# Down projection of a conv-FFN: separate buffers for the seven-product units, and another order of the units

## The chip, the cores and the metric

The kernel runs on one core of one Trainium2 chip. The metric is the time of one execution on the device in microseconds (us), as the median of several runs. Alongside it stands one profiled execution, whose trace gives every instruction with its start, its duration and what it waited for.

Engines are named as the profile names them: PE (TensorE, matrix products; PEld is its weight load), DVE (VectorE), ACT (ScalarE), POOL (GpSimd) and SP (SyncE, which here only issues DMAs; SPq is its queue).

## The reference

One decoder layer on 256 tokens of width 2048, all in float32: an attention mixer with a residual, then a gated FFN with a causal convolution. Only the second half matters here:

```python
a, b = jnp.split(h @ w_up, 2, axis=-1)          # w_up: 2048 x 11264
c = conv_b + sum(conv_w[j] * ap[:, j:j + S] for j in range(3))
y = (gelu(c) * b) @ w_down                      # w_down: 5632 x 2048
out = x + rms_norm(y, norm_ffn_post)
```

In what follows G stands for `gelu(c) * b`, 256 tokens by 5632 columns, and "down" for the product of G with `w_down`.

## The kernel before

**Numbers.** Each float32 operand is split in two parts, a high part `hi` (float32r, written by ACT with a cast) and a low part `lo` (the difference, written by DVE). A product of two operands is three matmuls (lines 175 to 177): high by high, high by low, low by high. One of them covers 128 rows by 128 columns against 512 columns.

**Weights.** A weight chunk of 128 partitions by 1024 floats (512 KB) goes through four hands. SP issues its load into a tile `raw`, of which there are three (`RAW = 3`, tag "raw"). ACT casts it to `whi` (L143), DVE subtracts to get `wlo` (L144), and PE reads both. Once both L143 and L144 have read a raw tile, it is free for the next load. Of converted pairs (`whi`, `wlo`) five can be outstanding in this stage (four, and one in two flexible tiles). `wchunk` loads and converts in one step. In the down stage the loads are issued by `raw_row` (L151), and `convert` does the other two steps.

**Stages around the change.** `ffn_up(c, ...)` makes 512 columns of G at a time. Columns 1 to 5 are made first, as k-tiles 4 to 23, after column 0 in `ffn_up0`. Then `down_pair(0)` and `down_pair(1)` multiply k-tiles 0 to 23 with `w_down`, each for one half (1024) of its columns, and add the result into `dsum` (tiles `ds`). Then `ffn_up` makes columns 6 to 10 in the same G tiles, and `down` finishes k-tiles 24 to 43, followed by the post-FFN norm with its scale `gpost2` (`z_block`, L1174) and the residual.

**Inside `down_pair`.** Twenty-four k-tiles are twelve units of two k-tiles each. Eight are plain: for each k-tile a row of weights is loaded and converted, and multiplied for two token halves and two column halves, so that a k-tile takes 4 products and a plain unit 24 matmuls. Four units (u = 0 to 3) use a scheme of seven products instead of eight (a Strassen-like one), 21 matmuls. Such a unit loads both its rows (`even`, `odd`), forms four differences of 128x512 on DVE (L1124 to L1127) in two further tiles `ta` and `tb`, and converts `odd`, half of `even`, `ta` and `tb`. Both raw rows are held until the last difference (L1127) and their conversions are done. `PAIR_ORDER` gives the order: `p` a plain unit, `s` a unit of seven. The products go to eight PSUM banks: four are called `c` and collect all units, and four are called `q` and collect products of the seven-units alone. At the last seven-unit of a pair (`if last`) one ACT copy and four DVE adds (L1141 to L1145) move `q` into `dsum`. After the whole pair, four adds (L1155) take in `c`. Pair 1 uses the banks of pair 0 the other way around, and the next `ffn_up` writes first (tile `ua`, L1041) into the banks that were `q` in pair 1.

**What sets the order.** The program is written as steps in the order of PE's work. The framework then gives each engine a fixed order by priority and by its own estimate of when inputs are ready; an instruction can be taken ahead of others where the estimate has its engine idle. On the chip each engine, and SP's queue among them, works through its list in order and stands at a semaphore until the inputs are there. Tiles of one tag follow one another in program order: the next one may be written when all readers of the one before are done.

**The tag "gp".** One tile of 128x2048 floats (1 MB in all). First it holds `gpost`, the scale after the mixer, whose last reader is L858. Then it holds `gpost2`, loaded by one broadcast DMA from POOL (L1077), and first read by L1174.

**x2b.** The residual is parked in DRAM and loaded back by eight DMAs on SP (`unpark`, L1013), each 256 KB. Its tiles are held until then by the token sums `s` of the seven-units, the first for units 0 and 1, the second for units 2 and 3.

Of the kernel before, what the change touches and what calls it, by code (L numbers as in the profile page):

```python
# [19 lines left out]
P = 128  # L20
D = 2048
# [20 lines left out]
def trunk_layer(ctx, tc, x, x_cols_in, conv_cols_in, g_mix_post, g_ffn_post, w_in, w_q, w_kv,  # L42
                sinks, rel, wo_a, wo_b, w_out, w_up, w_down, rope_tab, strip_sel, out):
    nc = tc.nc
    vec, act, pe, pool = nc.vector, nc.scalar, nc.tensor, nc.gpsimd

    def open_pool(name, bufs=1, **kw):
        es = ExitStack()
        return es, es.enter_context(tc.tile_pool(name=name, bufs=bufs, **kw))
# [9 lines left out]
    def sb(pl, shape, name, dt=F32, tag=None, bufs=None):  # L59
        return pl.tile(shape, dt, name=name, tag=tag or name, **({"bufs": bufs} if bufs else {}))  # L60
# [46 lines left out]
    def ring_tile(kind, name, dt, extra):  # L107
        pl_tag = dict(name=name, tag="flex", bufs=2) if extra else dict(name=name, tag=kind, bufs=RAW if kind == "raw" else RING)
        return ring.tile([P, 1024], dt, **pl_tag)

    def in_turn(kind):

        turn[kind] += 1
        return flex[0] == kind and turn[kind] % (RAW + 2 if kind == "raw" else RING + 1) >= (RAW if kind == "raw" else RING)
# [32 lines left out]
    def raw_row(src):  # L147
        i = cnt[0]
        cnt[0] += 1
        raw = ring_tile("raw", f"raw{i}", F32, in_turn("raw"))  # L150
        nc.sync.dma_start(raw, src)  # L151
        return raw
# [4 lines left out]
    def at(t, *fs):  # L157
        steps[max(t, now[0])].extend(fs)
# [20 lines left out]
    def gemm(xh, xl, w, k0, nk, c0, n, split=None, extra=None, ps=None):  # L179

        kc = 1024 // n if n in (256, 512) else 2
        acc = new_acc("g", ps)
        todo = []
        cuts = list(range(0, nk, kc)) + [nk]
        for ci, (k, ke) in enumerate(zip(cuts[:-1], cuts[1:])):
            kk = ke - k
            src = w[(k0 + k) * P:(k0 + k + kk) * P, c0:c0 + n].rearrange("(a p) n -> p a n", p=P)
            hi, lo = wchunk(src, [kk, n], *(extra or {}).get(ci, ()))
            for j in range(kk):
                kt = k + j  # L190
                wh, wl = hi[:, j * n:(j + 1) * n], lo[:, j * n:(j + 1) * n]
                for t in range(NT):
                    x_ = [x(k0 + kt)[:, t * P:(t + 1) * P] for x in (xh, xl)]
                    if split is None or t == 0 or ci < split:
                        mm3(acc[t][:, :n], *x_, wh, wl, kt == 0, kt == (split * kc if split and t else nk) - 1)
                    else:
                        todo.append((kt, x_, wh, wl))
            tick()
        return acc, todo
# [377 lines left out]
    acc, _ = gemm(XH, XL, w_in, 0, KT, 0, 512)  # L577
# [4 lines left out]
    acc, _ = gemm(XH, XL, w_in, 0, KT, C_KV, KVR + ROPE)  # L582
# [201 lines left out]
    for j in range(4):  # L784
        acc, _ = gemm(XH, XL, w_in, 0, KT, C_GA + 512 * j, 512)
# [15 lines left out]
    es6, p6 = open_pool("p6")  # L801
# [33 lines left out]
    for j in range(4):  # L835
        ld = merge_loads(j)
        acc, _ = gemm(AH, AL, wo_a, 0, KT, 512 * j, 512)
# [124 lines left out]
    def ffn_up0():  # L962

        sa = [[None, None], [None, None]]

        def evac(acc, q):
            f = sb(p6, [P, 1024], f"f{q}_0", tag="f" + "ab"[q], bufs=2)
            for t in range(NT):
                a = f[:, t * 512:(t + 1) * 512]
                act.activation(a, acc[t], AF.Copy, scale=rf[t][q][:, 0:1])  # L970
                sa[t][q] = a

        def cols(i):
            pt = pst.tile([P, 512], F32, name=f"fT{i}", tag="t")
            for q in range(2):
                for t in range(NT):
                    pe.transpose(pt[:, q * 256 + t * P:q * 256 + (t + 1) * P], sa[t][q][:, i * P:(i + 1) * P], ident)
            conv_cols(i, pt[:, 0:256], pt[:, 256:512], i)

        acc, todo = gemm(HH, HL, w_up, 0, KT, 0, 512, split=0, extra=first_extra)  # L980
        finish_tile(acc[1], todo)
        x2_norm(0)
        x2_norm(1)
        evac(acc, 0)
        drain()
        es8.close()
        esx.close()
        es7, p7 = open_pool("p7")
        g = [slot("b", i) if i < 8 else sb(p7, [P, 1024], f"ghl{i}", F32R) for i in range(12)]
        gT[0][:], gT[1][:] = highs(g), lows(g)  # L990
        dsum_all[:] = [sb(p7, [P, D], f"ds{t}") for t in range(NT)]
        dsum[:] = [[d[:, j * 512:(j + 1) * 512] for j in range(4)] for d in dsum_all]
        norm_row()
        for p in range(8):
            at(now[0] + 1 + (3 * p) // 2, lambda p=p: normed(p, p7))
        acc, _ = gemm(HH, HL, w_up, 0, KT, DFF, 512, ps=(pss, "s"))
        evac(acc, 1)
        for i, w in enumerate((1, 2, 4, 6)):
            at(now[0] + w, lambda i=i: cols(i))
        gtiles[:] = g  # L1000
        s_pool.append(p7)
        return es7
# [70 lines left out]
            at(now[0] + 1 + 2 * i, lambda i=i: conv_cols(4 * c + i, sa[0][i], sa[1][i], slot0 + i))  # L1073

    es7 = ffn_up0()
    gpost2 = sb(p6, [P, D], "gpost2", tag="gp")
    pool.dma_start(gpost2, g_ffn_post.partition_broadcast(P))  # L1077
    for c in range(1, 6):
        if c == 2:
            for i in range(8):  # L1080
# [15 lines left out]
    def down_pair(p):  # L1096

        c11, c12, c21, c22 = c = banks(p, f"c{p}_")
        q1, q5, q7, q6 = q = banks(1 - p, f"q{p}_")
        j0, used = 2 * p, set()  # L1100
        d = [dsum[t][j0 + j] for t in range(NT) for j in range(2)]
        act_of = lambda k, t: (GH(k)[:, t * P:(t + 1) * P], GL(k)[:, t * P:(t + 1) * P])
        row = lambda k: w_down[k * P:(k + 1) * P, j0 * 512:(j0 + 2) * 512]
        half = lambda w, i: tuple(x[:, i * 512:(i + 1) * 512] for x in w)

        def mul(o, x, w, last=False):
            mm3(o, *x, *w, id(o) not in used, last)
            used.add(id(o))

        def plain(u, last):  # L1110
            for k in (2 * u, 2 * u + 1):
                w = convert(raw_row(row(k)), 1024)
                for t in range(NT):
                    for j in range(2):
                        mul(c[2 * t + j], act_of(k, t), half(w, j), last and k % 2 == 1)
                tick()

        def seven(u, last):
            s1, s2, s3, s4 = s_of[u]
            even, odd = raw_row(row(2 * u)), raw_row(row(2 * u + 1))  # L1120
            ta, tb = (sb(p6, [P, 1024], f"t{n}{p}_{u}", tag="f" + n, bufs=2) for n in "ab")
            lo_, hi_ = slice(0, 512), slice(512, 1024)
            w = convert(odd, 1024)
            vec.tensor_tensor(ta[:, lo_], even[:, hi_], even[:, lo_], op=ALU.subtract)  # L1124
            vec.tensor_tensor(ta[:, hi_], odd[:, hi_], even[:, hi_], op=ALU.subtract)
            vec.tensor_tensor(tb[:, lo_], odd[:, hi_], ta[:, lo_], op=ALU.subtract)
            vec.tensor_tensor(tb[:, hi_], odd[:, lo_], tb[:, lo_], op=ALU.subtract)  # L1127
            mul(c11, act_of(2 * u + 1, 0), half(w, 0))
            mul(c12, s4, half(w, 1))
            w = convert(even, 512)  # L1130
            mul(q1, act_of(2 * u, 0), half(w, 0), last)
            w = convert(ta, 1024)
            mul(q5, s1, half(w, 0), last)
            mul(q7, s3, half(w, 1), last)
            tick()
            w = convert(tb, 1024)
            mul(q6, s2, half(w, 0), last)
            mul(c21, act_of(2 * u + 1, 1), half(w, 1))
            tick()
            if last:  # L1140
                act.copy(d[0], q1)  # L1141
                vec.tensor_tensor(d[1], d[0], q6, op=ALU.add)
                vec.tensor_tensor(d[2], d[1], q7, op=ALU.add)
                vec.tensor_tensor(d[3], d[2], q5, op=ALU.add)
                vec.tensor_tensor(d[1], d[1], q5, op=ALU.add)  # L1145

        plain_of, seven_of = iter(range(4, 12)), iter(range(4))
        for i, kind in enumerate(PAIR_ORDER):
            if kind == "s":
                u = next(seven_of)  # L1150
                seven(u, u == 3)
            else:
                plain(next(plain_of), i == len(PAIR_ORDER) - 1)
        for o, x in zip(d, c):
            vec.tensor_tensor(o, o, x, op=ALU.add)  # L1155

    for p in range(2):
        down_pair(p)
    for i in range(8):
        at(now[0] + 40 + 2 * i, lambda i=i: unpark(i // 4, i % 4))  # L1160
    for c in range(6, 11):
# [65 lines left out]


RING = 4
PAIR_ORDER = "psppsppsppsp"  # L1230
XCUT = [0, 1, 2, 3, 4, 6, 8, 10, 12, 14, 16]
X_LOAD = [0, 1, 2, 3, 4, 6, 7, 8, 10]
X_SQ = [4, 4, 5, 5, 6, 7, 8, 9, 10, 11]
# [71 lines left out]
```

## Time and profile before

| what | value |
|---|---|
| median of 3 runs | 1475.25 us (1474.59 to 1475.66) |
| time of the profiled execution | 1475.35 us |
| span of the profiled execution | 1473.5 us |
| granted TensorE clock | 0.998 |
| down stage, pair 0 (first matmul to first matmul of pair 1) | 1003.91 to 1066.47 us |
| down stage, pair 1 (to the first matmul of the next `ffn_up`) | 1066.47 to 1132.44 us |

All times of the trace count from the start of the span, which lies within the profiled execution's 1475.35 us with 1.85 us around it. In a row of groups the columns are: line, engine, operation, what is written and read, shape and count, then busy time and mean duration of one in ns, then idle time of the engine just before them and what ended it. In a timeline row they are start, duration, engine, line, operation, and in brackets idle time ahead and what released it. Waits give the total in us, how many times, and the longest. Chain rows give the start and the length of each step of the sequence that ended last. Window rows give for each stretch the busy time of PE, PEld, DVE, ACT and POOL with counts, then the granted clock, the DMA engines' busy share and GB/s.

The duration of a matmul in the trace is modelled: one of 512 columns is listed with 0.39 us, though one starts every 0.23 us. PE's busy time therefore hides a part of every short stop; the starts show it.

### The profile page before, as it was taken

Reading aid. Unit: us, or ns where it says so; the run is one execution under the profiler, and the core shown is the slowest. Engines: PE = TensorE matmul, PEld = TensorE weight load, DVE = VectorE, ACT = ScalarE, POOL = GpSimd, SP = SyncE. Lnnn points to the kernel's source line nnn. Section 1 sums busy time; section 2 is a strip of 40 time slices with the busy share of each in tenths; the row PEclk is TensorE's granted clock in tenths of the full one; section 3 lists DMA queues with packets and bytes.
Section 4 is the critical chain, followed back from the end, with each engine's and each line's share of the span. In section 5 each row is a group of like instructions: output and inputs, shape, how many; then the busy total and the mean of one; then the engine's idle time right before and its main releaser. Section 6 shows DMA issues by size and latency. Waiting matters only on the chain.

```text
span 1473.5 us, 20861 instructions
## 1 busy us (share of the span) xinstructions
PE 1460.6 (99%) x7591; PEld 1246.1 (85%) x7591; DVE 1026.6 (70%) x1799; ACT 818.3 (56%) x1354; POOL 51.1 (3%) x87
## 2 busy tenths in 40 slices
PE   9999999999999999999999999999999999999997
PEld 7888888888888888888888888888877888888886
DVE  7788874445667665555799877677777676677556
ACT  7588864444565554444666565555444565565443
POOL 0021100000000010000000000000000000000000
PEclk9999999999999999999999999999999999999999
DMA  8755376666655559755766666665667666666653
GB/s 291 223 171 165 94 219 195 206 209 200 186 160 156 171 163 339 224 197 195 224 202 184 192 193 185 188 196 162 209 199 226 210 200 190 194 186 187 198 189 126
DMA packets 154513, 287.58 MB, mean 195 GB/s; under 512 B 18427, under 2 KB 29596, under 8 KB 154284
## 3 DMA queue, kind: packets, MB, share of 16 engines
q1 hardware_dynamic: 149664, 270.43, 59.4%
q0 software_dynamic: 4656, 15.78, 3.4%
q8 instruction: 59, 0.97, 0.3%
q14 instruction: 42, 0.34, 0.1%
q10 hardware_dynamic: 92, 0.05, 0.0%
HBM read 277.79 MB, written 8.44 MB: 194 GB/s over the span
## 4 chain that ended last, share of the span: by engine, by line
PE 92%; DVE 3%; DMA 3%; ACT 1%; issue 0%; DVEq 0%; ACTq 0%; SPq 0%
PE accg L175 15%; PE accg L177 15%; PE accg L176 15%; PE ub L1041 10%; PE ua L1041 10%; PE ua L1045 5%; PE ub L1045 5%; DMA raw<-in_ffn_w_down_dram 2%; PE c L175 1%; PE c L176 1%; PE c L177 1%; DVE wlo L144 1%; PE mpo L760 1%; PE ms L726 1%; PE pt L442 1%; PE qn L691 1%
## 5 line engine op out<-in xcount | busy, mean ns | idle before, releaser
L144 DVE TENSOR_TENSOR wlo<-raw,whi 128x1024 fp32r<-128x1024 f32 (+2 forms) x502 | 604.7, 1207 | 345.4 <-ACT whi L143 340.6
L143 ACT CAST whi<-raw 128x1024 fp32r<-128x1024 f32 (+2 forms) x502 | 518.6, 1036 | 495.7 <-PE accg L177 239.2
L175 PE MATMUL accg<-whi,ahl 128*128 128x512 f32 (+1 forms) x544 | 212.9, 391 | 0.0
L177 PE MATMUL accg<-whi,ahl 128*128 128x512 f32 (+1 forms) x544 | 210.5, 387 | 0.0
L176 PE MATMUL accg<-wlo,ahl 128*128 128x512 f32 (+1 forms) x544 | 209.7, 385 | 0.0
L175 PE MATMUL accg<-whi,bhl 128*128 128x512 f32 x442 | 173.0, 391 | 0.0
L177 PE MATMUL accg<-whi,bhl 128*128 128x512 f32 x442 | 172.3, 390 | 0.0
L176 PE MATMUL accg<-wlo,bhl 128*128 128x512 f32 x442 | 172.2, 390 | 0.0
L1041 PE MATMUL ua<-ahl,whi 128*128 128x512 f32 x640 | 154.8, 391 | 0.9 <-DVE ds L1145 0.9
L1041 PE MATMUL ub<-ahl,whi 128*128 128x512 f32 x640 | 154.6, 391 | 0.0
L1041 PEld LDWEIGHTS ua<-ahl,whi 128*128 128x128 f32 x640 | 117.4, 188 | 24.0 <-DVE ds L1145 1.3
L1041 PEld LDWEIGHTS ub<-ahl,whi 128*128 128x128 f32 x640 | 117.5, 188 | 22.9 <-ACT cc L930 0.3
L177 PEld LDWEIGHTS accg<-whi,ahl 128*128 128x128 f32 x544 | 102.1, 188 | 20.6
L176 PEld LDWEIGHTS accg<-wlo,ahl 128*128 128x128 f32 x544 | 102.3, 188 | 18.1
L175 PEld LDWEIGHTS accg<-whi,ahl 128*128 128x128 f32 x544 | 102.3, 188 | 17.9
L177 PEld LDWEIGHTS accg<-whi,bhl 128*128 128x128 f32 x442 | 83.0, 188 | 17.4
L175 PEld LDWEIGHTS accg<-whi,bhl 128*128 128x128 f32 x442 | 83.0, 188 | 16.9
L176 PEld LDWEIGHTS accg<-wlo,bhl 128*128 128x128 f32 x442 | 83.0, 188 | 16.8
L1045 PEld LDWEIGHTS ub<-ahl,wlo 128*128 128x128 f32 x640 | 82.2, 191 | 3.2
L1045 PEld LDWEIGHTS ua<-ahl,wlo 128*128 128x128 f32 x640 | 82.2, 191 | 3.1
L1045 PE MATMUL ua<-ahl,wlo 128*128 128x256 f32 x640 | 83.7, 283 | 0.0
L1045 PE MATMUL ub<-ahl,wlo 128*128 128x256 f32 x640 | 83.2, 283 | 0.0
(409 smaller groups left out, 1876.1 us busy)
## 6 DMA issues: line engine op xcount, KB each, us to landing
raw<-in_ffn_w_up_dram SPq DMA_DIRECT2D x176, 512.0 KB, 4.5
raw<-in_w_in_dram SPq DMA_DIRECT2D x111, 512.0 KB, 4.4
raw<-in_ffn_w_down_dram SPq DMA_DIRECT2D x88, 512.0 KB, 4.3
raw<-in_w_o_swa_dram SPq DMA_DIRECT2D x32, 512.0 KB, 4.3
raw<-in_w_o_mla_dram SPq DMA_DIRECT2D x32, 512.0 KB, 4.8
raw<-in_w_out_dram SPq DMA_DIRECT2D x32, 512.0 KB, 4.2
bias<-strip POOLq DMA_DIRECT2D x16, 256.0 KB, 4.3
raw<-in_mla_w_q_up_dram SPq DMA_DIRECT2D x32, 128.0 KB, 2.6
```

Of the source, the lines that this page charges most:

```text
L143: act.copy(hi[:, a:b], raw[:, a:b])
L144: vec.tensor_tensor(lo[:, a:b], raw[:, a:b], hi[:, a:b].bitcast(F32), op=ALU.subtract)
L175: pe.matmul(o, ah, bh, start=start, stop=False)
L176: pe.matmul(o, ah, bl, start=False, stop=False)
L177: pe.matmul(o, al, bh, start=False, stop=stop)
L442: pe.transpose(pt[:, j * P:(j + 1) * P], p[:, c * P:(c + 1) * P], ident)
L691: pe.matmul(o, wl, ch(k), start=False, stop=k == nk - 1)
L726: pe.matmul(o, w, v_, start=n == 0, stop=False)
L760: pe.matmul(o, w(t), p_[:, c], start=n == 0, stop=n == 5)
L1041: pe.matmul(acc[i], hi[:, c], hn[p][:, j * 512:(j + 1) * 512], start=p + j == 0, stop=stop)
L1045: pe.matmul(acc[i][:, 0:256], lo[:, c], hn[p][:, j * 512:j * 512 + 256], start=False, stop=False)
```

## The change

Three edits. First, a unit of seven no longer takes its two rows from the three `raw` tiles. It allocates one tile of 128x2048 with the tag "gp" and loads its two rows into the halves. Second, `gpost2` is allocated and loaded after both pairs, since the same tile serves the eight seven-units in between. Third, `PAIR_ORDER` becomes a pair of orders, one for each column pair. Both end in two plain units; before, both ended in one.

```diff
     es7 = ffn_up0()
-    gpost2 = sb(p6, [P, D], "gpost2", tag="gp")
-    pool.dma_start(gpost2, g_ffn_post.partition_broadcast(P))
     for c in range(1, 6):
...
         def seven(u, last):
             s1, s2, s3, s4 = s_of[u]
-            even, odd = raw_row(row(2 * u)), raw_row(row(2 * u + 1))
+            both = sb(p6, [P, D], f"rr{p}_{u}", tag="gp")
+            even, odd = both[:, 0:1024], both[:, 1024:2048]
+            nc.sync.dma_start(even, row(2 * u))
+            nc.sync.dma_start(odd, row(2 * u + 1))
...
-        for i, kind in enumerate(PAIR_ORDER):
+        for i, kind in enumerate(PAIR_ORDER[p]):
             if kind == "s":
                 u = next(seven_of)
                 seven(u, u == 3)
             else:
-                plain(next(plain_of), i == len(PAIR_ORDER) - 1)
+                plain(next(plain_of), i == len(PAIR_ORDER[p]) - 1)
...
     for p in range(2):
         down_pair(p)
+    gpost2 = sb(p6, [P, D], "gpost2", tag="gp")
+    pool.dma_start(gpost2, g_ffn_post.partition_broadcast(P))
...
-PAIR_ORDER = "psppsppsppsp"
+PAIR_ORDER = ("ppsppspspspp", "psppsppspspp")
```

## Prediction

> **What bounds the kernel now.** I read the page first, then PE in the two column pairs by windows and by its starts, then the waits, then the chain that ended last. The page:
>
> ```profile
> span 1473.5 us, 20861 instructions
> PE 1460.6 (99%) x7591; PEld 1246.1 (85%) x7591; DVE 1026.6 (70%) x1799; ACT 818.3 (56%) x1354; POOL 51.1 (3%) x87
> ```
>
> PE is the bound nearly everywhere, so the change can only win what PE loses in the down stage. Windows of the two pairs, and PE's starts in them:
>
> ```profile
> 1003.91:1066.47 62.56, 62.56 (x278) 51.80 (x276) 50.04 (x63) 32.43 (x40) 0.00 (x0) 1.00 0.60 190
> 1066.47:1134.20 67.73, 65.01 (x281) 51.87 (x279) 49.91 (x57) 31.18 (x33) 0.00 (x0) 1.00 0.65 201
> ```
>
> ```profile
> 1003.91 0.39 PE L175 MATMUL c<-whi,bhl 128*128 128x512 f32 x1
> ...
> 1066.47 0.39 PE L175 MATMUL c<-whi,bhl 128*128 128x512 f32 x1
> ...
> 1076.08 0.50 PE L176 MATMUL q<-wlo,s 128*128 128x512 f32 x1 [0.16 <-DVE wlo L144]
> ...
> 1089.52 0.50 PE L176 MATMUL c<-wlo,bhl 128*128 128x512 f32 x1 [0.82 <-DVE wlo L144]
> ...
> 1122.02 0.50 PE L176 MATMUL c<-wlo,bhl 128*128 128x512 f32 x1 [0.80 <-DVE wlo L144]
> ...
> 1132.44 0.84 PE L1041 MATMUL ua<-ahl,whi 128*128 128x512 f32 x3
> 1134.20 0.50 PE L1041 MATMUL ua<-ahl,whi 128*128 128x512 f32 x1 [0.92 <-DVE ds L1145]
> ```
>
> A pair is 8 x 24 + 4 x 21 = 276 matmuls. Pair 0 takes 62.56 us, 0.2267 us for each, and no row in it has a bracket: it runs at PE's pace. Pair 1 does the same work in 65.97 us (1066.47 to 1132.44), **3.40 us** more, where PE waited for a low part of the weights. The three matmuls that follow end the pace at 1132.44 + 3 x 0.2267 = 1133.12; the next starts at 1134.20, **1.08 us** late, because L1145 still read the bank. Together 4.48 us, which is 0.30% of the time. The brackets alone give 2.70 us, the rest hides in the modelled ends. At the clock of 1.00 nothing else can be won here.
>
> Why is the low part late in pair 1 and not in pair 0? The waits of both pairs (the first two of DVE and ACT's side, the others of SP's queue):
>
> ```profile
> ACT whi L143 <- DMA raw<-in_ffn_w_down_dram: 52.2, 27, 5.5
> ...
> DVE ta L1125 <- DMA raw<-in_ffn_w_down_dram: 9.4, 6, 2.8
> ```
>
> ```profile
> SPq L151 <- DVE wlo L144: 51.5, 27, 5.5
> SPq L151 <- DVE tb L1127: 19.7, 7, 5.1
> ```
>
> ACT waits for loads, and SP waits for free buffers: a loop through three raw tiles, two of which a seven-unit holds until L1127. The chain shows one turn of that loop whole, from one L1127 to the next:
>
> ```profile
> 1104.49 0.69 DVE tb L1127
> 1105.17 0.61 DVE wlo L144
> ...
> 1105.80 5.27 DMA raw<-in_ffn_w_down_dram
> ...
> 1111.17 1.06 ACT whi L143
> ...
> 1112.26 1.24 DVE wlo L144
> ...
> 1113.51 6.00 DMA raw<-in_ffn_w_down_dram
> ...
> 1119.53 0.69 DVE ta L1125
> 1120.22 0.60 DVE tb L1126
> 1120.82 1.14 DVE wlo L144
> 1121.96 0.61 DVE tb L1127
> ```
>
> ```profile
> L1127 DVE TENSOR_TENSOR tb<-raw,tb x8: 682/684/686, 1005.5 to 1121.9; 128x512 f32<-128x512 f32 x8
> ```
>
> Two loads in series. Eight L1127 lie 116.4 us apart, 16.63 us a turn; PE needs only (21 + 48) x 0.2267 = 15.64 us for a seven-unit and two plain ones. So the supply falls back 0.99 us a turn, 6.9 us in seven turns. It starts with a lead:
>
> ```profile
> 1007.96 1.23 DVE L144 TENSOR_TENSOR wlo<-tb,whi 128x1024 fp32r<-128x1024 f32 x1 [0.29 <-ACT whi L143]
> ```
>
> ```profile
> 1012.98 0.39 PE L176 MATMUL q<-wlo,s 128*128 128x512 f32 x1
> ```
>
> The first `wlo` of `tb` is ready at 1009.19 and used at 1012.98, a lead of 3.8 us. 6.9 less 3.8 is 3.1, near the 3.40 found. The lead is used up in pair 0, and pair 1 pays.
>
> **The change part by part.**
>
> *Rows of the seven-units in their own tile.* Loads, casts, differences and matmuls stay the same in number: 48 loads, 552 matmuls. What changes is which buffer each waits for. There are now two loops beside each other. The rows they are made from, besides the chain above, are SP's issues with the time to landing, and the DVE groups of this stage:
>
> ```profile
> L151 SPq DMA_DIRECT2D raw<-in_ffn_w_down_dram x48: 327/328/643, 986.1 to 1122.6; - x48
> ...
> DMA to landing us min/median/max: 3.5/4.4/6.0
> ```
>
> ```profile
> L144 DVE TENSOR_TENSOR wlo<-raw,whi 128x1024 fp32r<-128x1024 f32 x39 | 47.5, 1222 | 18.0 <-ACT whi L143 17.5
> ...
> L1127 DVE TENSOR_TENSOR tb<-raw,tb 128x512 f32<-128x512 f32 x8 | 5.5, 684 | 0.0
> ...
> L144 DVE TENSOR_TENSOR wlo<-raw,whi 128x512 fp32r<-128x512 f32 x7 | 4.8, 687 | 0.1
> ```
>
> (a) The seven-unit's tile: L1127 ends, SP issues two loads (0.33 us for the first), the second lands 4.4 to 6.0 us later, then L1125, L1126, a `wlo` and L1127 (0.69 + 0.60 + 1.14 + 0.61 = 3.04). That is 7.8 to 9.4 us; one load in series where there were two. (b) The three raw tiles serve plain rows only: a load (3.5 to 6.0) and its conversion (1.06 + 1.24) are 5.8 to 8.3 us for three rows, at most 2.8 a row. (c) DVE: a seven-unit is 4 x 0.684 + 3 x 1.222 + 0.687 = 7.1 us, a plain one 2 x 1.222 = 2.4.
>
> *The order.* From seven-unit to seven-unit there are now three short turns (one plain unit between, 45 x 0.2267 = 10.20 us of PE: two late in pair 0, one late in pair 1), three of 15.64, and one across the pairs of 21.1 (three plain units). In a short turn loop (a) asks 7.8 to 9.4 of the 10.20, loop (b) at most 5.5, DVE 9.5; in one of 15.64 they ask 9.4, 11.1 and 12.0. All are under PE's need, DVE and loop (a) in the short turns by only 0.7 to 0.8 us. So the lead holds, and the 3.40 us go. Next late after the stall would be DVE in the short turns.
>
> [...]
>
> *Two plain units at the end.* The last `q` matmul of pair 1 and the adds that free its banks:
>
> ```profile
> L177 PE MATMUL q<-whi,s x24: 387/389/393, 1011.8 to 1126.1; 128*128 128x512 f32 x24
> ```
>
> ```profile
> 1133.54 0.61 DVE ds L1145
> ```
>
> From 1126.1 to 1134.15 is 8.1 us, because the adds stand in DVE's queue between conversions that wait for loads. PE covered 5.4 us with one plain unit and some products of the last seven; with two it covers 5.44 more. Even the unchanged 8.1 us are then hidden: **1.08 us** goes. In DVE's queue, conversions stand behind these adds and behind the four of L1155, as before; the up to five converted pairs cover them.
>
> *gpost2 later.* Its issue before, and its first reader:
>
> ```profile
> 738.03 0.54 POOL L1077 DMA_DIRECT2D gpost<-in_norm_ffn_post_dram x1 [8.74 <-DVE ry_u L222]
> ```
>
> ```profile
> L1174 DVE TENSOR_TENSOR ds<-ds,gpost x6: 684/684/686, 1385.9 to 1440.9; 128x512 f32<-128x512 f32 x6
> ```
>
> It moves to after the last L1127 of pair 1, near 1112, some 270 us ahead of its reader, on POOL, which does nothing from there on (0.00 in the windows). It costs nothing by itself. But 1 MB then meets the loads of x2b for units 2 and 3 (1 MB) and four plain rows (2 MB) within 10.9 us. The busiest stretch seen near there:
>
> ```profile
> 1132.50:1140.00 7.50, 6.58 (x37) 5.45 (x36) 6.30 (x9) 3.14 (x3) 0.00 (x0) 1.00 0.87 303
> ```
>
> 303 GB/s at a share of 0.87 put the ceiling near 348; 4.2 MB take 12.0 us, 1.2 us over. The lead of 3.8 covers that; without it, 1.2 us are lost.
>
> *The first rows into "gp"* may be loaded any time after `gpost` is free, when POOL's load was. On SP they stand among the loads of the up projection. If they stand there as long as POOL did, 8.74 us, nothing is lost either: SP stood longer already between 690 and 800 us, where PE's waits show nothing.
>
> ```profile
> SPq L131 <- DVE wlo L144: 72.4, 30, 11.2
> ```
>
> **Sum.** Bounds: nothing to 4.48 us gained, if no new wait comes. I keep a remnant of 0.2 for the interruption at 1076, where L1155's adds still stand ahead of a seven-unit's conversions. 1475.35 - 4.28 is 1471.1 for the profiled execution; the median is 0.10 lower, so I forecast **1471.0 us**.
>
> **The rivals.**
>
> *SP's order costs the short turns* (chance 0.12). If SP has the two "gp" loads ahead of the plain rows between two seven-units, these rows wait for L1127 too. The turn is then 1.3 for four issues, 6.0 to land, 2.3 to convert the plain row and 3.04, 12.7 us, 2.5 over PE's 10.20. Two such in pair 0 lose 5.0, less the lead of 3.8, 1.2 us; pair 1 has the lead again by then. Time 1470.8 + 1.2 = 1472.0. For it: SP waited 19.7 us on L1127 before. Against: plain rows come first in the program and their tiles come free first. [...]
>
> *The same, slower than before* (0.06). All raw loads of the kernel, not these alone, show:
>
> ```profile
> DMA to landing us min/median/max: 2.2/4.3/9.3
> ```
>
> With 9.3 for 6.0 that turn is 16.0 us. Pair 0 loses 2 x 5.8 - 3.8 = 7.8; the 21.1 restores the lead, two turns of 15.64 take 0.7 of it, and pair 1 loses 5.8 - 3.1 = 2.7. Time 1470.8 + 10.5 = 1481.3. It decides from a turn of 14.2 us, where 3 x (14.2 - 10.20) - 2 x 3.8 equals 4.48. Against: landings here never passed 6.0.
>
> *Loads crowd at the end* (0.05): the 1.2 us above, 1472.0.
>
> *The supply doesn't speed up* (0.07), since SP's list keeps the old pace; then only the end wins, 1475.25 - 1.08 = 1474.2.
>
> **How the numbers follow.** The forecast has the remaining 0.70. Its own range is 1470.1 (all 4.48 and the 0.66 by which the lowest run lay below the median) to 1471.5. The full range goes up over both cases at 1472.0 and the spread of the runs: 1470.0 to 1472.8; it leaves out 0.13 and a tail of the rest. A measurement of this kernel can tell about 0.2% from no change, 2.95 us, so faster means under 1472.3: the forecast and somewhat over half of the two cases at 1472.0, 0.78. Slower 0.07; same 0.15.
>
> **What would show it.** Right: pair 1 spans 62.6 us from its first matmul to the first of `ua`, with no bracket from L144 or L1145; L1127 starts lie about 15.6 and 10.2 us apart, at PE's pace; ACT's wait for `w_down` loads shrinks from 52.2 us and its wait for PE grows from 4.4. Wrong: brackets after the second and third short turn (SP's order), or a turn still near 16.6 (no faster supply), or a bracket near `ua` with x2b and the scale in flight (crowding). A PE wait outside the down stage would be an effect I have not priced.

## The result

The changed kernel takes 1480.27 us (median of 7 runs, 1477.35 to 1485.04) against 1474.59 us (7 runs, 1474.40 to 1475.66): the ratio is 1.0043, with a 95% interval of 1.0026 to 1.0059. It is **slower**, by 0.4%, and its times spread over 7.7 us where those of before spread over 1.3. The forecast was 1471.0.

The profiled execution took 1480.16 us, with a span of 1477.9. Lines 1125 to 1128 of the changed kernel are the differences that stood at 1124 to 1127 before. First the windows of the two pairs in it, the second up to the first matmul of `ua`:

```profile
1004.17:1068.48 64.31, 63.15 (x278) 51.66 (x276) 50.33 (x66) 33.89 (x42) 0.00 (x0) 1.00 0.53 175
1068.48:1138.07 69.59, 66.28 (x278) 53.61 (x277) 48.98 (x54) 30.80 (x33) 0.54 (x1) 0.95 0.64 213
```

Pair 0, which lost nothing before, now takes 1.74 us more than PE needs, and pair 1 takes 7.02 us more. From the first matmul of the stage to the first of `ua` are 133.90 us. The 552 matmuls need 125.14 at 0.2267 each, so 8.76 us are lost, where 3.39 were before, and 1.08 behind them, which are now gone. That makes 4.3 of the 4.8 us between the two profiled executions. And the granted clock, 1.00 everywhere in the stage before, is 0.95 in the second window. PE's starts show the pauses (start, duration, engine, line, what; in brackets the idle time ahead and what ended it):

```profile
1046.61 0.50 PE L176 MATMUL c<-wlo,ghl 128*128 128x512 f32 x1 [0.57 <-DVE wlo L144]
...
1057.69 0.50 PE L176 MATMUL c<-wlo,ghl 128*128 128x512 f32 x1 [0.59 <-DVE wlo L144]
...
1079.87 0.50 PE L176 MATMUL q<-wlo,s 128*128 128x512 f32 x1 [2.17 <-DVE wlo L144]
...
1082.34 0.80 PE L176 MATMUL c<-wlo,bhl 128*128 128x512 f32 x1 [0.77 <-DVE wlo L144]
1082.93 0.63 PE L177 MATMUL c<-whi,bhl 128*128 128x512 f32 x1
...
1117.04 0.50 PE L176 MATMUL c<-wlo,ghl 128*128 128x512 f32 x1 [0.38 <-DVE wlo L144]
```

Every pause is for a low part, `wlo`, which DVE writes. Yet the supply of weights did improve. In the waits (who waits for whom, total, times, longest), ACT's wait for loads of `w_down` is down from 52.2 us, and its wait for PE, which means that it is ahead, is up from 4.4. First the row of before, then three of the change:

```profile
ACT whi L143 <- PE c L177: 4.4, 5, 1.5
```

```profile
ACT whi L143 <- PE c L177: 30.5, 24, 2.6
ACT whi L143 <- DMA raw<-in_ffn_w_down_dram: 20.0, 7, 5.3
DVE ta L1125 <- DMA rr<-in_ffn_w_down_dram: 16.1, 6, 4.1
```

The last row is the one to follow: six times DVE stands at the first difference of a seven-unit, for the unit's rows. DVE's timeline around the longest pause shows what stands behind it:

```profile
1076.77 0.69 DVE L1125 TENSOR_TENSOR ta<-rr 128x512 f32<-128x512 f32 x1 [2.55 <-DMA rr<-in_ffn_w_down_dram]
1077.99 0.69 DVE L1126 TENSOR_TENSOR ta<-rr 128x512 f32<-128x512 f32 x1 [0.53 <-DMA rr<-in_ffn_w_down_dram]
1078.60 1.22 DVE L144 TENSOR_TENSOR wlo<-tb,whi 128x1024 fp32r<-128x1024 f32 x1
1079.74 0.68 DVE L1127 TENSOR_TENSOR tb<-rr,ta 128x512 f32<-128x512 f32 x1
```

The differences are those of the *next* seven-unit, u = 1 of pair 1. The `wlo` of `tb` at 1078.60 belongs to the *present* one, u = 0, whose last matmul ahead of the pause started at 1077.32; at its pace PE needed that `wlo` at 1077.55 and had it at 1079.82. Its cast had been ready since 1072.23, and DVE was idle for 2.55 us with it in its queue. The rows came late for this reason (the release of the tile on DVE, then SP's issues):

```profile
1070.01 0.69 DVE L144 TENSOR_TENSOR wlo<-rr,whi 128x512 fp32r<-128x512 f32 x1
```

```profile
1070.72 0.33 SPq L1120 DMA_DIRECT2D rr<-in_ffn_w_down_dram  x1
1071.10 0.43 SPq L1121 DMA_DIRECT2D rr<-in_ffn_w_down_dram  x1
```

The single tile is free when the last conversion that reads it is done, at 1070.70. SP issues at once, and DVE can start on the first row some 6 us later, at 1076.77. The framework had put the difference ahead of that `wlo`, presumably because its own estimate had the row landed by then; no run shows that estimate. Each of the other four pauses also follows a stand of DVE at L1125, with the low part that PE needs behind it.

Behind the pause of 2.17 us the clock falls. Windows of the changed kernel; the last three numbers are granted clock, DMA share and GB/s:

```profile
1080.00:1082.30 2.30, 1.56 (x6) 0.92 (x6) 2.27 (x4) 1.05 (x1) 0.00 (x0) 0.80 0.00 0
1082.30:1088.10 5.80, 5.76 (x14) 4.56 (x15) 3.98 (x4) 1.63 (x2) 0.00 (x0) 0.50 0.76 238
1088.10:1092.00 3.90, 3.90 (x18) 3.21 (x17) 1.51 (x3) 1.05 (x1) 0.00 (x0) 0.99 0.70 245
```

The mean of 0.80 in the first window puts the fall to 0.50 near 1081.4: 1.5 us after PE had started again, and no later than the start of the pause of 0.77 us, which therefore did not cause it. From 1082.34 to 1088.05 thirteen matmuls take 5.71 us, 2.76 more than at full clock. That is more than the longest pause itself, and almost two thirds of the 4.3 us that the change added in this execution.

### The profile page after: what moved, and what is told of

The parts are those of the page before. It is cut to its first block, busy times and chain, and to the rows that moved or that the text cites. A ratio compares the mean times of both kernels' runs of the same rounds, so it can differ in the third digit from the quotient of the medians.

```text
span 1477.9 us, 20854 instructions
## 1 busy us (share of the span) xinstructions
PE 1463.6 (99%) x7591; PEld 1248.9 (85%) x7591; DVE 1026.2 (69%) x1799; ACT 820.0 (55%) x1354; POOL 51.1 (3%) x87
## 4 chain that ended last, share of the span: by engine, by line
PE 91%; DVE 4%; DMA 3%; ACT 1%; issue 1%; SPq 0%; DVEq 0%; ACTq 0%
PE accg L175 15%; PE accg L177 15%; PE accg L176 15%; PE ub L1041 10%; PE ua L1041 10%; PE ub L1045 5%; PE ua L1045 5%; DMA rr<-in_ffn_w_down_dram 2%; DVE wlo L144 2%; PE c L176 1%; PE c L177 1%; PE c L175 1%; DMA raw<-in_ffn_w_down_dram 1%; PE mpo L760 1%; PE ms L726 1%
## 5 line engine op out<-in xcount | busy, mean ns | idle before, releaser
L144 DVE TENSOR_TENSOR wlo<-raw,whi 128x1024 fp32r<-128x1024 f32 (+2 forms) x486 | 589.0, 1215 | 339.7 <-ACT whi L143 332.2
L143 ACT CAST whi<-raw 128x1024 fp32r<-128x1024 f32 (+2 forms) x486 | 505.8, 1043 | 474.1 <-PE accg L177 240.3
L177 PE MATMUL accg<-whi,ahl 128*128 128x512 f32 (+1 forms) x544 | 210.4, 387 | 0.0
L177 PE MATMUL accg<-whi,bhl 128*128 128x512 f32 x442 | 172.3, 390 | 0.0
L177 PEld LDWEIGHTS accg<-whi,ahl 128*128 128x128 f32 x544 | 102.1, 188 | 20.5
L177 PEld LDWEIGHTS accg<-whi,bhl 128*128 128x128 f32 x442 | 83.0, 188 | 17.2
```

Of the source, the lines that this page charges most:

```text
L143: act.copy(hi[:, a:b], raw[:, a:b])
L144: vec.tensor_tensor(lo[:, a:b], raw[:, a:b], hi[:, a:b].bitcast(F32), op=ALU.subtract)
L177: pe.matmul(o, al, bh, start=False, stop=stop)
```

## The experiments

**Theory A**: low parts that PE needs stand on DVE behind a difference that waits for its rows, and the rows are late, since the single tile is reloaded only after its last conversion. **Rivals**: B, loads into the single tile stand in SP's queue and hold up plain rows; C, the loop through the single tile is too slow whatever DVE's order; O, the orders of the units cost by themselves. "Lost" below is PE's time from the stage's first matmul to the first of `ua`, less 125.14 us. The experiments ran in two series, each with the kernel before in it.

| kernel | median us | runs | against before | lost in its profile, us |
|---|---|---|---|---|
| before | 1474.8 and 1474.6 in the two series | 26, 20 | | 3.39 (+ 1.08 behind) |
| changed | 1480.27 | 7 | 1.0043 (1.0026 to 1.0059) | 8.76 |
| orders alone | 1476.05 | 11 | 1.0012 (1.0003 to 1.0021) | 6.30 |
| tile alone | 1477.68 | 10 | 1.0019 (1.0010 to 1.0028) | 8.58 |
| changed, differences pinned | 1471.66 | 11 | 0.9979 (0.9970 to 0.9988) | 0.0 |
| changed, rows from POOL | 1483.57 | 5 | 1.0060 (1.0047 to 1.0072) | 12.34 |
| tile alone, pinned | 1471.21 | 10 | 0.9974 (0.9964 to 0.9983) | 0.03 |
| before, pinned | 1485.75 | 5 | 1.0070 (1.0058 to 1.0083) | 15.13 |
| orders alone, pinned | 1484.66 | 5 | 1.0069 (1.0055 to 1.0083) | 11.34 |
| ring of five | 1473.49 | 11 | 0.9993 (0.9984 to 1.0002) | 1.51 |

**The orders alone.** Rows stay in the three raw tiles.

```diff
-PAIR_ORDER = "psppsppsppsp"
+PAIR_ORDER = ("ppsppspspspp", "psppsppspspp")
```

> Only the new orders; the rows of the seven-units stay in the three raw tiles and the post-FFN scale is loaded early, as before. Theory A (DVE's fixed order has the first difference of the next seven-unit, L1125, ahead of low parts that PE needs next; its rows come late, because the single tile comes free only with its last conversion; a long pause of PE then lowers the granted clock) and its rivals B (loads into the single tile stand in SP's queue and hold up the plain rows) and C (the serial loop through the single tile is too slow in the short turns, whatever the order on DVE) all need the new tile, so all expect no more loss than before here: the supply loss of about 3.4 us stays, the 1.08 us at the first matmuls of the next up projection go, 1473.5 us (1472.5 to 1475). If the short turns cost by themselves (theory O), it is 1477 or more, with pauses in the last third of each pair.

1476.05 us, slightly slower than before, between the two expectations. The two long pauses came at pair 1's beginning, after the two short turns of pair 0, and behind the longer one the clock fell in the profiled execution (1478.59 us; a mean of 0.66 from 1079 to 1084), so that it overstates the usual loss:

```profile
1078.18 0.50 PE L176 MATMUL c<-wlo,bhl 128*128 128x512 f32 x1 [2.00 <-DVE wlo L144]
```

With three tiles the new orders cost a little, 1.3 us; they don't explain the 5.7 us of the change.

**The tile alone.** The change with the old order in both pairs.

```diff
-PAIR_ORDER = ("ppsppspspspp", "psppsppspspp")
+PAIR_ORDER = ("psppsppsppsp", "psppsppsppsp")
```

> The new tile and the late scale, but the old order in both pairs, so that every turn from seven-unit to seven-unit has two plain units (15.64 us of PE). A: DVE still stands at L1125 for the rows, but these have 5.4 us more, so pauses are shorter and the clock stays at 1.00: 1472 to 1475 us. B: much the same, SP's waits hold up plain rows by less. C: the loop of under 12 us fits in 15.64, so the supply loss of 3.4 us goes and only the 1.08 us at the end stay: 1471.9. O: all the harm is gone, 1472 or less.

1477.68 us: slower than before without any short turn. C and O fail here, both wanted 1472 or less. A's mechanism is there, with more harm than I gave it (1475 us at most, and a clock that stays at 1.00, where the mean from 1113 to 1118 is 0.66): DVE stands at L1125 for 16.7 us in six waits, the longest 5.7, and PE pauses for 2.79 us in one piece:

```profile
1112.63 0.50 PE L176 MATMUL q<-wlo,s 128*128 128x512 f32 x1 [2.79 <-DVE wlo L144]
```

**The differences pinned.** The changed kernel; on DVE the first two differences come in program order, behind the unit's first conversion. Loads, tiles and orders of units are the change's own.

```diff
-            vec.tensor_tensor(ta[:, lo_], even[:, hi_], even[:, lo_], op=ALU.subtract)
-            vec.tensor_tensor(ta[:, hi_], odd[:, hi_], even[:, hi_], op=ALU.subtract)
+            tc.keep_in_program_order(vec.tensor_tensor(ta[:, lo_], even[:, hi_], even[:, lo_], op=ALU.subtract))
+            tc.keep_in_program_order(vec.tensor_tensor(ta[:, hi_], odd[:, hi_], even[:, hi_], op=ALU.subtract))
```

> The changed kernel, with the first two differences of a seven-unit (L1125, L1126) kept in program order on DVE, so behind the conversions of the units before it. Nothing else is changed; loads, tiles and orders are those of the change. A: no low part stands behind a difference that waits for a load, PE's pauses go and so does the lowered clock: 1470.5 to 1472.5 us. B and C: the rows come as late as before, PE pauses as long: 1477 to 1483, with DVE's wait at L1125 turned into PE's wait for the low part of ta.

1471.66 us, 8.6 less than the changed kernel and 3.1 less than before. Its windows show both pairs at PE's pace:

```profile
1004.93:1067.49 62.56, 62.56 (x278) 51.82 (x276) 53.79 (x70) 34.15 (x42) 0.00 (x0) 1.00 0.57 187
1067.49:1130.05 62.56, 62.56 (x278) 51.82 (x276) 47.90 (x53) 30.33 (x32) 0.54 (x1) 1.00 0.69 230
```

On DVE the same unit's `tb` is now converted ahead of the next unit's difference, which finds its rows there and has no bracket:

```profile
1072.05 1.22 DVE L144 TENSOR_TENSOR wlo<-tb,whi 128x1024 fp32r<-128x1024 f32 x1
1074.26 3.72 DVE L144 TENSOR_TENSOR wlo<-raw,whi 128x1024 fp32r<-128x1024 f32 x3 [0.99 <-ACT whi L143]
...
1081.64 0.68 DVE L1125 TENSOR_TENSOR ta<-rr 128x512 f32<-128x512 f32 x1
```

So A holds as a whole, and C falls a second time: one tile is enough. But the pin does two things at once. The low parts no longer stand behind the difference, and the tile comes free sooner: on DVE the conversion of half of `even` now stands ahead of the last difference. SP's waits show it, the first row from the change, the second with the pin:

```profile
SPq L1120 <- DVE wlo L144: 6.8, 6, 1.9
```

```profile
SPq L1120 <- DVE tb L1128: 23.4, 6, 7.7
```

In the change the last conversion ended 0.6 us behind the last difference in three units and 4.0 to 9.6 in the four others ahead of a reload. ACT's and SP's lists shift in a few places too (two loads of x2b move ahead of one unit's rows). Which part of the 8.6 us belongs to which of these, no run tells.

**Rows from POOL.** The changed kernel with the two row loads on POOL's queue.

```diff
-            nc.sync.dma_start(even, row(2 * u))
-            nc.sync.dma_start(odd, row(2 * u + 1))
+            pool.dma_start(even, row(2 * u))
+            pool.dma_start(odd, row(2 * u + 1))
```

> The changed kernel, with the two loads of a seven-unit's rows issued from POOL's queue, which has nothing else to do in this stage; SP's queue holds the plain rows and x2b alone. B: plain rows are no longer held up, PE's pauses go: 1470.5 to 1473 us. A: the rows still wait for the tile to come free and DVE still stands at L1125 with low parts behind it: pauses of 1 to 3 us stay, 1476 to 1483. C: as A.

1483.57 us, slower still, and just above A's range. B falls: with SP's queue clear of these loads the pauses are more, each of A's kind. From DVE's, POOL's and PE's timeline:

```profile
1110.91 0.53 POOL L1120 DMA_DIRECT2D rr<-in_ffn_w_down_dram  x1 [18.60 <-DVE wlo L144]
...
1116.75 0.69 DVE L1125 TENSOR_TENSOR ta<-rr 128x512 f32<-128x512 f32 x1 [5.00 <-DMA rr<-in_ffn_w_down_dram]
1117.36 1.22 DVE L144 TENSOR_TENSOR wlo<-tb,whi 128x1024 fp32r<-128x1024 f32 x1
...
1118.63 0.50 PE L176 MATMUL q<-wlo,s 128*128 128x512 f32 x1 [1.74 <-DVE wlo L144]
```

Why it is slower than the change itself I did not pursue; its DVE waits for the rows are longer (21.3 us at L1125 against 16.1).

**The tile alone, pinned.** The old order, the new tile, the pin of above.

> The tile alone with the old order (as the run of the tile alone, 1477.7 us), plus the two differences kept in program order on DVE. Theory A (low parts that PE needs stand on DVE behind a difference that waits for its load): the pauses in the pairs go, only the late adds at the end may stay (1.08 us): 1471.5 to 1473 us. Rival O (the orders of the units decide, the old one is the better or the worse by itself): it differs from the changed kernel with the same pin (1471.7) by over 2 us either way.

1471.21 us, as good as with the new orders (1471.66, whose runs cover it). The stage loses 0.03 us, and `ua` starts without a break though one plain unit stands at the end. The orders are worth nothing measurable once the low parts come on time; the 1.08 us at the end go without the second plain unit too.

**Before, pinned**, and **the orders alone, pinned**: the same two lines in kernels with three raw tiles for all rows.

> The kernel before, with nothing but the two differences kept in program order on DVE. Reading R (the prediction's: three raw tiles bound the supply at 16.63 us a turn): no change, 1474 to 1476 us, or slightly slower, as differences come later. Reading D (DVE's order was behind the loss before the change too: while DVE stands at a difference, conversions that would free raw tiles stand behind it): the 3.4 us of pair 1 go and the 1.08 at the end stay or go, 1470.5 to 1472.5.

> The new orders alone (three raw tiles for all rows; 1476.05 us without a pin), with the pin. R: the supply through three tiles is what loses, 1474.5 to 1477. D: with the pin the three tiles are enough, 1470.5 to 1472.5, as with the new tile.

1485.75 and 1484.66 us, about 10 slower than before. D falls. Reading R holds as to direction, but its ranges are missed by 8 to 10 us; that the pin would cost so much I had not expected. With three tiles ACT still waits for loads, its casts now wait for the late differences too, and PE makes many short pauses. Waits of the pinned kernel of before:

```profile
ACT whi L143 <- DMA raw<-in_ffn_w_down_dram: 46.1, 26, 5.6
ACT whi L143 <- DVE ta L1125: 13.3, 6, 2.6
PE q L176 <- DVE wlo L144: 5.5, 9, 0.8
```

That these waits make up the 10 us is argued from them and was not tested.

**A ring of five.** The change's orders without the pin; the 1 MB is cut in two tiles of 512 KB, which take turns with the three raw tiles for all rows.

```diff
-            both = sb(p6, [P, D], f"rr{p}_{u}", tag="gp")
...
+            even, odd = ring_row(row(2 * u)), ring_row(row(2 * u + 1))
...
+    def ring_row(src):
+        rows[0] += 1
+        if rows[0] % 5 < 3:
+            return raw_row(src)
+        r = sb(p6, [P, 1024], f"rr{rows[0]}", tag="gp", bufs=2)
+        nc.sync.dma_start(r, src)
+        return r
```

> The changed kernel's orders, but the 1 MB of the single tile is cut in two halves that join the three raw tiles: each row of the stage, plain or of a seven-unit, takes the next of five tiles in turn, so a seven-unit's rows are loaded well ahead. No pin. A: a difference that doesn't wait for its load harms nobody; pauses go or stay under 1 us together, 1471 to 1473 us. If lateness of the rows isn't needed for the harm (the order on DVE delays low parts anyhow): 1475 or more.

1473.49 us, between the two expectations: 6.8 less than the change with the same orders of units. PE has one pause worth the name, of 0.79 us, and loses 1.51. But DVE stands at differences nearly as long as in the change, 14.4 us over four rows of its waits against 17.2 over two. So it is not simply that rows come early: with five tiles for all rows more is converted ahead (ACT waits 35.4 us for PE at L177, against 30.5 in the change, and 9.8 for loads of `w_down`, against 21.8), and a stand of DVE does less harm. Which share each has, this run doesn't tell; a second tile of 1 MB, which would, was not tried. Against before, no difference shows (0.9984 to 1.0002).

**The changed kernel twice more**, one execution each.

> The changed kernel itself, one more profiled execution. If the spread of its times (1477.35 to 1485.04 us) comes from pauses of PE that differ from one execution to the next and from a lowered clock behind the longest of them, the sum of what PE loses in the two pairs follows the time: about 6 us lost at 1477.5, 8.8 at 1480.2, 13 at 1485, with every pause on a low part. If the loss is alike and the time is not, the spread is from elsewhere.

> As the run before this one: a third profiled execution of the changed kernel, to see where the pauses fall and whether the granted clock drops behind one of over 2 us again, as it did in the first (0.50 behind a pause of 2.17 and one of 0.77 us).

1478.39 us with 6.51 lost, and 1478.53 with 6.77: time follows loss. Pauses fall in part at the same places, with other lengths (in the first of the two 0.26 and 0.80 us, where the execution above had 2.17 and 0.77), none is over 1.2 us, and the clock stays at 1.00. Two of the first one's:

```profile
1080.94 0.50 PE L176 MATMUL c<-wlo,bhl 128*128 128x512 f32 x1 [0.80 <-DVE wlo L144]
...
1097.99 0.50 PE L176 MATMUL c<-wlo,bhl 128*128 128x512 f32 x1 [1.12 <-DVE wlo L144]
```

So without a fallen clock the change is still some 4 us slower than the median of before. The stage accounts for 2.0 and 2.3 us of the 3.0 and 3.2 by which these two executions exceed the profiled one of before; most of the rest lies ahead of the stage, whose first matmul came 0.8 and 0.6 us later. The lowered clock adds to it in some executions. That the slowest (1485.04) had it worse is a guess; it was not profiled.

## Why the prediction was wrong

*What bounds the kernel.* Right. PE has a floor of 125.1 us in the stage; two kernels reached it, and their medians (1471.2 and 1471.7) lie near the forecast of 1471.0, which the change itself missed.

*Why before loses 3.4 us.* Supported. With the tile, ACT's wait for loads falls from 52.2 to 20.0 us, and with tile and pin the loss is nil. The pin alone, with three tiles, makes it worse, so with this pin the tile is needed; other orders on DVE with three tiles were not run.

*The step that failed* is in "Rows of the seven-units in their own tile" and "The order": "All are under PE's need, DVE and loop (a) in the short turns by only 0.7 to 0.8 us. So the lead holds, and the 3.40 us go." It compared what loops and engines can carry and took it that each engine does its work in the order in which PE wants it. But the change gives DVE a new wait, at L1125 for rows that are reloaded late, and I never asked what stands behind it. There stood the `wlo` of the unit that PE was at. The traces of before could have warned: DVE had waited 9.4 and 2.3 us at L1125 and L1124 there, and I read these rows only as a sign of slow loads. The second of them, in the kernel before:

```profile
DVE ta L1124 <- DMA raw<-in_ffn_w_down_dram: 2.3, 4, 0.8
```

In the source the pin changes nothing but the place of these two differences, and the loss goes from 8.76 us to none.

*A second fault in loop (a)*: it let the tile go at the last difference (L1127, in the change L1128). In the change a conversion frees it, which DVE did up to 9.6 us later. SP's issues into the tile lay 13.9 and 12.5 us apart around the first short turns of pair 0 (1024.23, 1038.17, 1050.66), where loop (a) asked 9.4 and PE's pace 10.20. With the pin the last difference frees the tile in six reloads, as loop (a) had it, and the same issues lie 12.0 and 10.6 us apart. So this fault too is one of DVE's order.

*Two plain units at the end.* The 1.08 us went. With three tiles and the new orders no break shows at `ua` either, so the second plain unit was enough, as the sum had it; but it was not needed, since with one plain unit and the new tile there is no break, with or without the pin.

*gpost2 later, the first rows into "gp", loads crowding at the end*: no cost, as priced; no bracket near `ua`, and nothing around 740 us.

*The rivals.* "SP's order" is refuted by the rows on POOL; in the change, too, SP stood at L1120 for a conversion for only 6.8 us in six waits. Its slower form gave 1481.3; that this lies near the result of 1480.27 is luck, since its mechanism did not occur. A rival with the new wait on DVE was missing, and so was the clock: I priced a pause at its own length, while the clock that fell behind one of 2.17 us cost another 2.76.

## What to carry to other kernels

When a buffer is added or moved, ask of each engine with a fixed order what stands behind the instruction that reads it, and not just whether loads and engines can carry the rate: a stand of 2.55 us on DVE, which is busy for 69% of the changed kernel's span, stopped PE, which is busy for 99% of it, for 2.17 us. Where a framework puts helper work that waits for a load ahead of the work that the bottleneck needs next, try pinning it behind. And test the pair, not the parts: the tile alone was 0.2% slower than before and the pin alone 0.7%, both together 0.26% faster.

## What the runs showed of the hardware

The granted clock fell to 0.50 in four of the twelve traces of the stage: behind a pause of 2.17 us in the change, of 2.00 with the orders alone, of 2.79 with the tile alone, and behind two of 0.75 and 0.77 us, 1.7 us apart, in the pinned kernel of before. Windows that hold the whole low part, in this order:

```profile
1080.00:1090.00 10.00, 9.23 (x28) 7.03 (x29) 7.48 (x8) 2.67 (x3) 0.00 (x0) 0.66 0.51 164
```

```profile
1079.00:1084.00 5.00, 5.00 (x16) 3.57 (x15) 4.43 (x5) 2.00 (x2) 0.00 (x0) 0.66 0.64 188
```

```profile
1113.00:1118.00 5.00, 4.84 (x15) 3.40 (x14) 5.00 (x7) 1.04 (x1) 0.00 (x0) 0.66 0.38 105
```

```profile
1134.00:1139.00 5.00, 4.40 (x12) 3.51 (x13) 3.63 (x4) 3.31 (x5) 0.00 (x0) 0.66 0.80 228
```

In the first, from 1081.4 to 1088.2, the granted clock is 0.50, and most matmuls start 0.42 to 0.43 us apart, against 0.2267 at 1.00. So they do in the low parts of the other three. A mean of 0.66 is then 0.50 for 6.8 us in the first and, as an estimate from these starts, for 3.4 us in each of the others, behind last pauses of 2.00, 2.79 and 0.77 us. The fall came when PE was at work again, 1.5, 1.4, 0.9 and 0.1 us after the last pause ahead of it had ended. But pauses alike did nothing elsewhere: one of 2.15 us in the kernel with rows from POOL, with nothing near it, and three of 0.76, 0.77 and 0.77 us within 4.2 us in the pinned kernel of before itself:

```profile
1062.00:1068.00 6.00, 6.00 (x28) 4.94 (x27) 6.00 (x9) 1.82 (x2) 0.00 (x0) 1.00 0.81 256
```

```profile
1110.00:1118.00 8.00, 5.60 (x22) 3.44 (x21) 6.71 (x9) 4.61 (x5) 0.00 (x0) 1.00 0.48 152
```

So the length of a pause alone does not decide. Nor does the sum of pauses close together: in the pinned kernel of before the clock fell behind two of 1.52 us in all, and stayed at 1.00 behind three of 2.30 us in all. What else decides was not shown: no run moves a pause to test it.
